# A state-space stage re-pipelined over three periods in a fixed order of TensorE and VectorE, its power products in fewer, longer VectorE operations

## The chip, the cores and the metric

The kernel runs on one core of one Trainium2 chip. A core has a matrix engine (TensorE, PE in the profile), a vector engine (VectorE, DVE), an activation engine (ScalarE, ACT), a general one (GpSimd, POOL) and one whose queue issues most transfers (SyncE, SP). Each takes its instructions in order; they wait for one another through semaphores. The metric is the device time of one execution in microseconds (us), median of several runs.

## What is computed

The reference is a trunk of two layers on x (512 positions, 1024 features, float32). Each normalises x, scales and shifts it by a condition, applies a mixer and adds the gated result. Layer 1's mixer is a gated DeltaNet, which the change doesn't touch. Layer 0's is a state-space mixer of 128 groups with 16 channels and 64 complex states each, cut to what matters:

```
u, z = split(h @ w_in)                      # 1024 -> 2 x 2048
dt = exp(log_dt); a = exp(lam * dt)         # complex; 64 states per group
bb = ((a - 1) / lam) * b                    # complex
x[t] = a * x[t-1] + bb @ u[t]               # per group, 512 positions
y = real(c @ x) + d * u
y = gelu(y); y = y * sigmoid(y @ w_glu); y = y * silu(z); out = y @ w_out
```

## The kernel before

Wide products (`mm3`, L90 to L93) run on TensorE as three passes over a pair of high and low parts: hi·hi, hi·lo, lo·hi. Each weight tile `wraw` (512 KB) is loaded by SP, rounded to `whi` by ScalarE (L78), and VectorE forms the remainder `wlo` (L79).

The kernel's part before 66.5 us makes h and the first eight column tiles of u. Then comes the state-space stage, up to about 429 us. It weaves two things. The first are 40 *units* (`unit`, L497): 24 column tiles of w_in (u to memory, then z through Silu and to memory) and 16 of the first half of w_glu. A unit is eight *fill steps* of three 128x512 matmuls each. Unit 24 on need the gelu of the first eight tiles of y (`p`), split in hi and lo (`yAhi`, `yAlo`); they are loaded back from memory, and their gelu runs, all eight together, at unit 23 (L499 to L505).

The second are sixteen *steps*, each for eight groups. The four positions of a block of four are folded into the contraction, so the recurrence runs over 128 blocks with a to the power 4. A step has
- `s5_prep` (L359): `bl`, the input products: powers of a (`wt`, two pieces loaded from `wd`) times b (`bB`), on GpSimd (L373 to L376), masked by ScalarE (L379); `ca`, the output products `xs`, `xt` of c and powers `pw` on VectorE, six operations of 256 elements (L393 to L398), copied to `cl` by ScalarE; the angles `tau`, on ScalarE (L408), reduced to a fraction in two VectorE operations (L409, L410), then sine and cosine on ScalarE; every fourth step `s5_quad`, the tile `bb` (six VectorE operations).
- `s5_front` (L419): the matmuls `v` of bl and u (L427), on VectorE the rotation into the frame of the decaying modulus (L434, L435), sums (L436, L437), two scans (L439), the rotation back (L442, L443) and the state `st` (L444, L445).
- `s5_back` (L449): the matmuls `y` of ca and state (L457), `kc` on VectorE, `kin` on ScalarE, the transposes `kt` (L467), their copies `tl` on ScalarE (L470), `out` (the product within a block, L473), `yb` and its store to `yd`.

The loop (L531 to L552) puts four units ahead, then in each of 17 periods sixteen fill steps, with the previous step's kt and out and this step's v among them. This order is the order of the program; the order on each engine is made from it by the tile scheduler, which moves instructions by its own cost estimates. After the loop the sixteen fill steps that are left run to the end (`fill(400)`), then the second half of y is loaded, put through gelu (`load_gelu`, L489) and split; its first matmul is `ps_g`.

Of the kernel before, what the change touches and what calls it, by code (L numbers as in the profile page):

```python
# [18 lines left out]
P = 128  # L19
T = 512  # L20
# [21 lines left out]
def hybrid_kernel(ctx: ExitStack, tc: tile.TileContext, a, out, dbg=None):  # L42
# [26 lines left out]
    eps_c, hpi_c = cols[:, 0:1], cols[:, 1:2]  # L69
# [77 lines left out]
    wd = dpool.tile([2, 4, 2, 64, 64], F32, name="wd")  # L147
# [19 lines left out]
    pw = sp.tile([P, 4, 2, 64], F32, name="pw")  # L167
# [9 lines left out]
    def s5_params():  # L177
# [53 lines left out]
        V.tensor_copy(qT[:, 0:2, :], vq[:, :, 64:P])  # L231
        V.tensor_scalar(out=qT[:, 2, :], in0=vq[:, 0, 64:P], scalar1=-1.0, scalar2=None, op0=ALU.mult)
        V.memset(vq[:, 0, 64:P], 1.0)
        V.memset(vq[:, 1, 64:P], 0.0)
        V.tensor_copy(pw[:, 0], vq[:, :, 64:P])
        ta = tmp2()
        tb = tmp2()
        for e in range(1, 5):
            v2 = tmp2()
            V.tensor_tensor(out=ta, in0=vq, in1=av[:, 0:1, :].to_broadcast([P, 2, P]), op=ALU.mult)  # L240
            V.tensor_tensor(out=tb, in0=vq, in1=av[:, 1:2, :].to_broadcast([P, 2, P]), op=ALU.mult)
            V.tensor_tensor(out=v2[:, 0, :], in0=ta[:, 0, :], in1=tb[:, 1, :], op=ALU.subtract)
# [69 lines left out]
    cl = [zz.tile([P, 2, 4, P], F32, name=f"cl{i}") for i in range(2)]  # L312
# [9 lines left out]
    def big(m):  # L322
        ps = psm.tile([P, T], F32, tag="mm", name="ps_mm")
        whi, wlo = load_w(a["winb"][m - 8])
        for k in range(KT):
            mm3(ps, whi[:, k * P:(k + 1) * P], wlo[:, k * P:(k + 1) * P], hhi[:, k, :], hlo[:, k, :],
                k == 0, k == KT - 1)
            if k < KT - 1:
                yield
        if m < 16:  # L330
            put_u(m, ps)
        else:
            z = up.tile([P, T], F32, tag="u", name="z")
            big.last = S.activation(out=z, in_=ps, func=AF.Silu).ins
            SY.dma_start(szd[m - 16], z)

    quad = {}

    def s5_quad(n):
        cC = s5.tile([P, 2, 16, 16], F32, tag="cC", name="cC")  # L340
        bT = s5.tile([P, 2, 16, 16], F32, tag="bT", name="bT", bufs=1)
# [11 lines left out]
        for c in range(2):
            V.tensor_tensor(out=ys[0], in0=bT[:, c], in1=q_b((0, 2)[c]), op=ALU.mult)
            V.tensor_tensor(out=ys[1], in0=bT[:, 1 - c], in1=q_b(1), op=ALU.mult)
            V.tensor_tensor(out=bb[:, c], in0=ys[0], in1=ys[1], op=ALU.subtract)
        return cC, dm, bb

    def s5_prep(i):  # L359
        par = i % 2  # L360
        if i % 4 == 0:
            quad[0] = s5_quad(i // 4)
        cC, dm, bb = quad[0]
        q4 = slice(4 * (i % 4), 4 * (i % 4) + 4)
        wt = s5.tile([P, 2, 256], F32, tag="wt", name="wt", bufs=1)
        for c in range(2):
            SY.dma_start(wt[:, c, :], wd[c].rearrange("j g q n -> (j g) (q n)")[:, 256 * i:256 * i + 256]
                         .unsqueeze(1).to_broadcast([8, 16, 256]))
        bB = s5.tile([P, 2, 256], F32, tag="bB", name="bB")
        SY.dma_start(bB, a["bB"].rearrange("p (c n) -> p c n", c=2)[:, :, 256 * i:256 * i + 256])  # L370
# [6 lines left out]
        bl = s5.tile([P, 2, 4, 2, 64], F32, tag="bl", name="bl")  # L377
        for g in range(2):
            S.activation(out=bl[:, :, :, g, :], in_=ta.rearrange("p c (q n) -> p c q n", n=64), func=AF.Copy,  # L379
                         scale=gmask[g])  # L380

        qs = slice(4 * i, 4 * i + 4)
        pwv = pw[:, :, :, qs].rearrange("p e c q -> p c q e")

        def c_b(c):
            return cC[:, c, q4, :].unsqueeze(2).to_broadcast([P, 4, 4, 16])

        def p_b(c):
# [5 lines left out]
        V.tensor_tensor(out=xt[:, 0], in0=c_b(1), in1=p_b(1), op=ALU.mult)
        V.tensor_tensor(out=xs[:, 0], in0=xs[:, 0], in1=xt[:, 0], op=ALU.subtract)
        V.tensor_tensor(out=xs[:, 1], in0=c_b(0), in1=p_b(1), op=ALU.mult)
        V.tensor_tensor(out=xt[:, 1], in0=c_b(1), in1=p_b(0), op=ALU.mult)
        V.tensor_tensor(out=xs[:, 1], in0=xs[:, 1], in1=xt[:, 1], op=ALU.add)  # L398
        for g in range(2):
            r = slice(64 * g, 64 * g + 64)  # L400
            S.copy(cl[par].rearrange("p c q (e g m) -> p c (q e) g m", e=4, g=2)[r, :, :, g, :],
                   xs[r].rearrange("p c q e m -> p c (q e) m"))
        S.copy(st[par][:, :, :, P:], bb[:, :, q4, :])

        tau = s5.tile([P, 4, P], F32, tag="tau", name="tau", bufs=1)
        kr = s5.tile([P, 4, P], F32, tag="kr", name="kr", bufs=1)
        for q in range(4):
            S.activation(out=tau[:, q, :], in_=iota, func=AF.Copy, scale=t4[:, 4 * i + q:4 * i + q + 1])  # L408
        V.tensor_scalar(out=kr, in0=tau, scalar1=RND, scalar2=RND, op0=ALU.add, op1=ALU.subtract)  # L409
        V.tensor_tensor(out=tau, in0=tau, in1=kr, op=ALU.subtract)  # L410
        tc_ = s5.tile([P, 4, P], F32, tag="tcos", name="tcos")
        ts_ = s5.tile([P, 4, P], F32, tag="tsin", name="tsin")
        S.activation(out=ts_, in_=tau, func=AF.Sin, scale=TWO_PI_LO)
        S.activation(out=kr, in_=tau, func=AF.Abs)
        S.activation(out=tc_, in_=kr, func=AF.Sin, scale=-TWO_PI_LO, bias=hpi_c)
        S.copy(r4t[par][:, :, 1:P], r4[:, qs].unsqueeze(2).to_broadcast([P, 4, P - 1]))
        return bl, tc_, ts_, dm[:, q4, :]

    def s5_front(i, bl, tcs, tsn):  # L419
        par = i % 2  # L420
        U = s5.tile([P, 4, P], F32, tag="U", name="U")
        for j in range(4):
            SY.dma_start(U[32 * j:32 * j + 32], ud[i].rearrange("(q r) (j b) -> j r q b", r=32, j=4)[j])
        psv = ps5.tile([P, 2, 4, P], F32, tag="v", name="ps_v")
        for c in range(2):
            for q in range(4):
                TE.matmul(psv[:, c, q, :], bl[:, c, q].rearrange("p g n -> p (g n)"), U[:, q, :], start=(q == 0), stop=(q == 3))  # L427
        za = s5.tile([P, 2, 4, P], F32, tag="za", name="za")
        zb = s5.tile([P, 2, 4, P], F32, tag="zb", name="zb", bufs=1)

        def flat(x):
            return x.rearrange("p q b -> p (q b)")
# [16 lines left out]
    def s5_back(i, U, dm):  # L449
# [16 lines left out]
        for q in range(4):  # L466
            TE.transpose(pkt[:, q, :], kin[:, q, :], ident)  # L467
# [783 lines left out]
```

## Time and profile before

| | |
|---|---|
| median of 3 runs | 1128.05 us (1125.78 to 1132.82) |
| the profiled execution | 1119.82 us |
| its span in the trace | 1118.1 us |
| TensorE busy | 1052.9 us, 94% |
| VectorE busy | 795.4 us, 71% |
| ScalarE busy | 572.6 us, 51% |
| GpSimd busy | 150.9 us, 13% |

The profile is of one execution. Its span runs from the first to the last instruction; the execution's time is 1.7 us longer. A window's row gives each engine's busy time in it, how many instructions, the clock granted to TensorE as a share of its full speed, the share of the DMA engines' time and what they moved. In a timeline a row gives start, duration, engine and line, operation, output and inputs, and in brackets how long the engine had been idle and for what it waited. The rows stand in a section of their own, below.

### The profile page before, as it was taken

Reading aid. Unit: us, or ns where it says so; the run is one execution under the profiler, and the core shown is the slowest. Engines: PE = TensorE matmul, PEld = TensorE weight load, DVE = VectorE, ACT = ScalarE, POOL = GpSimd, SP = SyncE. Lnnn points to the kernel's source line nnn. Section 1 sums busy time; section 2 is a strip of 40 time slices with the busy share of each in tenths; the row PEclk is TensorE's granted clock in tenths of the full one; section 3 lists DMA queues with packets and bytes.
Section 4 is the critical chain, followed back from the end, with each engine's and each line's share of the span. In section 5 each row is a group of like instructions: output and inputs, shape, how many; then the busy total and the mean of one; then the engine's idle time right before and its main releaser. Section 6 shows DMA issues by size and latency. Waiting matters only on the chain. (4 is left out here: it accounts for less than half of the span.)

```text
span 1118.1 us, 15281 instructions
## 1 busy us (share of the span) xinstructions
PE 1052.9 (94%) x5620; PEld 878.5 (79%) x5620; DVE 795.4 (71%) x1264; ACT 572.6 (51%) x1132; POOL 150.9 (13%) x126
## 2 busy tenths in 40 slices
PE   7997798888889999999999999999999999999997
PEld 5886677777768887888889877778888888887887
DVE  5998999999998747666777578679962344557253
ACT  4565576666877446333445556743343554434241
POOL 0014543232231000000001004220020000200000
PEclk9998899999999999999999999999998999999998
DMA  7766555545332349867664053232251101123342
GB/s 297 265 214 190 144 170 154 171 140 176 95 122 76 114 123 312 303 229 242 209 206 146 15 180 113 68 102 95 83 163 39 39 20 38 57 67 108 99 141 76
DMA packets 80316, 156.57 MB, mean 140 GB/s; under 512 B 9713, under 2 KB 39281, under 8 KB 80242
## 3 DMA queue, kind: packets, MB, share of 16 engines
q1 hardware_dynamic: 79234, 152.45, 41.7%
q0 software_dynamic: 1008, 3.15, 1.1%
q8 instruction: 44, 0.72, 0.3%
q14 instruction: 30, 0.25, 0.1%
HBM read 136.96 MB, written 18.61 MB: 139 GB/s over the span
## 5 line engine op out<-in xcount | busy, mean ns | idle before, releaser
L79 DVE TENSOR_TENSOR wlo<-wraw,whi 128x1024 fp32r<-128x1024 f32 (+1 forms) x141 | 173.0, 1227 | 120.5 <-ACT whi L78 107.3
L78 ACT CAST whi<-wraw 128x1024 fp32r<-128x1024 f32 (+1 forms) x141 | 141.0, 1000 | 209.3 <-PE ps_mm L92 88.3
L91 PE MATMUL ps_mm<-g_hhi,whi 128*128 128x512 f32 x360 | 149.0, 414 | 0.4 <-ACT whi L78 0.4
L92 PE MATMUL ps_mm<-g_hlo,whi 128*128 128x512 f32 x360 | 148.1, 411 | 0.0
L93 PE MATMUL ps_mm<-g_hhi,wlo 128*128 128x512 f32 x360 | 146.7, 408 | 0.5 <-DVE wlo L79 0.5
L93 PEld LDWEIGHTS ps_mm<-g_hhi,wlo 128*128 128x128 f32 x360 | 68.3, 190 | 14.7 <-DVE wlo L79 1.0
L91 PEld LDWEIGHTS ps_mm<-g_hhi,whi 128*128 128x128 f32 x360 | 68.2, 190 | 14.3 <-ACT whi L78 0.8
L91 PE MATMUL ps_mm<-hhi,whi 128*128 128x512 f32 x192 | 78.5, 409 | 0.0
L92 PEld LDWEIGHTS ps_mm<-g_hlo,whi 128*128 128x128 f32 x360 | 68.4, 190 | 12.7
L92 PE MATMUL ps_mm<-hlo,whi 128*128 128x512 f32 x192 | 75.9, 395 | 0.0
L93 PE MATMUL ps_mm<-hhi,wlo 128*128 128x512 f32 x192 | 75.3, 392 | 0.0
L457 PE MATMUL ps_y<-st,cl 128*128 128x144 f32 x256 | 43.9, 326 | 25.6 <-DVE st L444 24.1
L739 DVE SCALAR_TENSOR_TENSOR ac<-ps_mm,cw,ac 128x509 f32<-128x509 f32 (+2 forms) x87 | 64.8, 745 | 3.6 <-ACT ac L736 2.9
L457 PEld LDWEIGHTS ps_y<-st,cl 128*128 128x128 f32 x256 | 38.6, 216 | 33.1 <-issue 25.5
L102 DVE SCALAR_TENSOR_TENSOR adaw<-adaw,cact 128x1024 f32<-128x1024 f32 x48 | 58.8, 1229 | 5.1 <-DMA adaw<-in_adaw_dram 5.1
L128 POOL TENSOR_TENSOR rc<-rc,mhalf 128x2 f32<-128x2 f32 (+1 forms) x5 | 4.8, 960 | 391.8 <-DVE rc L127 378.0
L91 PE MATMUL ps_g<-yBhi,whi 128*128 128x512 f32 x128 | 50.7, 398 | 2.3 <-ACT yBhi L78 2.3
L91 PE MATMUL ps_gh<-yAhi,whi 128*128 128x512 f32 x128 | 51.7, 404 | 0.0
L93 PE MATMUL ps_g<-yBhi,wlo 128*128 128x512 f32 x128 | 50.5, 394 | 0.5 <-DVE wlo L79 0.5
L92 PE MATMUL ps_g<-yBlo,whi 128*128 128x512 f32 x128 | 50.4, 394 | 0.0
L92 PE MATMUL ps_gh<-yAlo,whi 128*128 128x512 f32 x128 | 50.2, 392 | 0.0
L93 PE MATMUL ps_gh<-yAhi,wlo 128*128 128x512 f32 x128 | 50.2, 392 | 0.0
(339 smaller groups left out, 2587.1 us busy)
## 6 DMA issues: line engine op xcount, KB each, us to landing
adaw<-in_adaw_dram SPq DMA_DIRECT2D x48, 512.0 KB
wraw<-in_wginb_dram SPq DMA_DIRECT2D x45, 512.0 KB
wraw<-in_wglu_dram SPq DMA_DIRECT2D x32, 512.0 KB
wraw<-in_winb_dram SPq DMA_DIRECT2D x24, 512.0 KB
wraw<-in_s5o_a_dram SPq DMA_DIRECT2D x16, 384.0 KB
wraw<-in_wgo_a_dram SPq DMA_DIRECT2D x16, 384.0 KB
wraw<-in_wina_dram SPq DMA_DIRECT2D x8, 512.0 KB
bB<-in_bB_dram SPq DMA_DIRECT2D x16, 256.0 KB
```

Source lines behind the costliest of these rows:

```text
L78: S.copy(hi, src)
L79: V.tensor_tensor(out=lo, in0=src, in1=hi.bitcast(F32), op=ALU.subtract)
L91: TE.matmul(ps, whi, xhi, start=start, stop=False)
L92: TE.matmul(ps, whi, xlo, start=False, stop=False)
L93: TE.matmul(ps, wlo, xhi, start=False, stop=stop)
L102: return V.scalar_tensor_tensor(out=aw, in0=aw, scalar=1.0, in1=cact, op0=ALU.mult, op1=ALU.mult, accum_out=mods[:, n:n + 1]).ins
L128: G.tensor_tensor(out=rc[:, 0:n], in0=rc[:, 0:n], in1=mhalf[:, 0:n], op=ALU.pow)
L457: TE.matmul(psy[q // 2][:, q % 2, :], cl[par][:, c, q, :], st[par][:, c, q, :], start=(q % 2 == 0 and c == 0), stop=(q % 2 == 1 and c == 1))
L739: V.scalar_tensor_tensor(out=ac[:, d:], in0=ps[:, 0:T - d], scalar=cw[:, n, k:k + 1], in1=ac[:, d:], op0=ALU.mult, op1=ALU.add)
```

## The change

The order of TensorE's and VectorE's instructions in the stage's loop is fixed by hand (`tc.manual_schedule`); ScalarE, SP and GpSimd are still ordered by the scheduler. A period now works on three steps: y, kt and out of the previous one, rotation, scan and state of the current one, and bl, fraction, sine, cosine, v and ca of the next. The bl products are three VectorE operations of 512 elements in place of four GpSimd ones; a third piece of `wt` and of `bB` (384 KB instead of 256) makes the sign part of the data. ca is three operations of 512, bb likewise. The rounding of the angle is an Identity activation with a bias on ScalarE, and the fraction one VectorE operation. Five units stand ahead of the first step instead of four, so that eight fill steps are left after the loop. Each tile `p` of the first half is loaded back in its own step instead of all at unit 23. U has three buffers instead of two; weight remainders and the casts have places in the order by hand. The diff, cut to its core:

```diff
-        wt = s5.tile([P, 2, 256], F32, tag="wt", name="wt", bufs=1)
+        s.wt = s5.tile([P, 3, 256], F32, tag="wt", name="wt", bufs=1)
...
-        G.tensor_tensor(out=ta, in0=bB, in1=wt[:, 0:1, :].to_broadcast([P, 2, 256]), op=ALU.mult)
-        G.tensor_tensor(out=tb, in0=bB, in1=wt[:, 1:2, :].to_broadcast([P, 2, 256]), op=ALU.mult)
-        G.tensor_tensor(out=ta[:, 0, :], in0=ta[:, 0, :], in1=tb[:, 1, :], op=ALU.subtract)
-        G.tensor_tensor(out=ta[:, 1, :], in0=ta[:, 1, :], in1=tb[:, 0, :], op=ALU.add)
+        V.tensor_tensor(out=ta, in0=s.bB[:, 0:2, :], in1=s.wt[:, 0:1, :].to_broadcast([P, 2, 256]), op=ALU.mult)
+        V.tensor_tensor(out=tb, in0=s.bB[:, 1:3, :], in1=s.wt[:, 1:3, :], op=ALU.mult)
+        V.tensor_tensor(out=ta, in0=ta, in1=tb, op=ALU.add)
...
-        V.tensor_scalar(out=kr, in0=tau, scalar1=RND, scalar2=RND, op0=ALU.add, op1=ALU.subtract)
-        V.tensor_tensor(out=tau, in0=tau, in1=kr, op=ALU.subtract)
+        S.activation(out=s.kr, in_=s.tau, func=AF.Identity, bias=rnd_c)
+    def s5_frac(s):
+        V.scalar_tensor_tensor(out=s.tau, in0=s.kr, scalar=RND, in1=s.tau, op0=ALU.subtract, op1=ALU.subtract)
...
-                for k in range(8):
-                    SY.dma_start(slot(8 + k), yd[k])
+        if s.i < 8:
+            SY.dma_start(slot(8 + s.i), yd[s.i])
...
-    fill(8 * 3)
+    fill(40)
...
+    with tc.manual_schedule(engines={mybir.EngineType.PE, mybir.EngineType.DVE}):
+        for i in range(17):
+            nxt = s5_load(i + 1) if i < 15 else None
+            if i in (1, 5, 9):
+                s5_quad((i + 3) // 4)
+            if prev:
+                s5_y(prev)
+            if cur:
+                s5_rot(cur)
+            fill(3)
+            if prev:
+                s5_kin(prev)
+            if cur:
+                s5_add(cur)
+                s5_cl(cur)
+            fill(1)
+            next_lo()
+            if prev:
+                s5_kt(prev)
+            if i == 9:
+                gelu_a(range(8))
+            if nxt:
+                s5_frac(nxt)
+                s5_bl(nxt)
+            fill(2)
+            if nxt:
+                s5_mask(nxt)
+            if cur:
+                s5_scan(cur)
+            fill(2)
+            unit_end()
+            if prev:
+                s5_out(prev)
+            if cur:
+                s5_unrot(cur)
+            fill(4)
+            if nxt:
+                s5_sincos(nxt)
+                s5_side(nxt)
+            if i < 14:
+                s5_angle(steps[i + 2])
+            if nxt:
+                s5_v(nxt)
+            if cur:
+                s5_state(cur)
+            next_lo()
+            if nxt:
+                s5_ca(nxt)
+            if i in (1, 5, 9):
+                s5_quad_b((i + 3) // 4)
+            fill(4)
+            unit_end()
+            prev, cur = cur, nxt
```

VectorE's order before, in one period of the middle of the stage (`za` and `zb` are the rotated products, `xs` and `xt` ca's products, `kc` the product within a block, `wlo` a weight remainder):

```order
L434 TENSOR_TENSOR za<-ps_v,tcos 128x1024
L435 TENSOR_TENSOR zb<-ps_v,tsin 128x1024
L393 TENSOR_TENSOR xs<-cC,pw 128x256
L436 TENSOR_TENSOR za<-za,zb 128x512
L437 TENSOR_TENSOR za<-za,zb 128x512
L395 TENSOR_TENSOR xs<-xs,xt 128x256
L439 SCALAR_TENSOR_TENSOR zb<-r4t_579,za 128x512 x2
L396 TENSOR_TENSOR xs<-cC,pw 128x256
L442 TENSOR_TENSOR zc<-zb,tcos 128x1024
L398 TENSOR_TENSOR xs<-xs,xt 128x256
L443 TENSOR_TENSOR zb<-zb,tsin 128x1024
L79 TENSOR_TENSOR wlo<-wraw,whi 128x1024
```

And after the change, at the same place, from rotation to back-rotation (the state, a second remainder and ca's three operations of 512 follow):

```order
L523 TENSOR_TENSOR za<-ps_v,tcos 128x1024
L524 TENSOR_TENSOR zb<-ps_v,tsin 128x1024
L558 TENSOR_TENSOR kc<-ps_y,dm 128x32 x2
L527 TENSOR_TENSOR za<-za,zb 128x512
L528 TENSOR_TENSOR za<-za,zb 128x512
L346 TENSOR_TENSOR wlo<-wraw,whi 128x1024
L461 SCALAR_TENSOR_TENSOR tau<-kr,tau 128x512
L479 TENSOR_TENSOR ta<-bB,wt 128x512
L480 TENSOR_TENSOR tb<-bB,wt 128x512
L481 TENSOR_TENSOR ta<-ta,tb 128x512
L532 SCALAR_TENSOR_TENSOR zb<-r4t_579,za 128x512 x2
L537 TENSOR_TENSOR zc<-zb,tcos 128x1024
```

ca has left the chain from the rotation to the state; kc, a remainder, the fraction and the three bl products stand between the sums and the scans instead. On ScalarE, before, the gelu of the first half stand together behind one load of the function table, with the casts of the split behind them:

```order
L505 ACT_TABLE_LOAD
L505 ACTIVATE p_2477<-p_2477 128x512
L505 ACTIVATE p_2479<-p_2479 128x512
L505 ACTIVATE p_2481<-p_2481 128x512
L505 ACTIVATE p_2483<-p_2483 128x512
L505 ACTIVATE p_2485<-p_2485 128x512
L505 ACTIVATE p_2487<-p_2487 128x512
L78 CAST yAhi<-p_2477 128x512
```

After, although the code writes all eight at i = 9, the scheduler puts one into each of the periods 2 to 9, and each has a table load ahead of it and one behind it, before the next Silu of z; this is the second of them:

```order
L560 ACTIVATE kin<-kc,cst 128x16x16 x2
L352 ACT_TABLE_LOAD
L352 ACTIVATE p_1346<-p_1346 128x512
L569 COPY tl_575<-ps_kt 32x512
L569 COPY tl_575<-ps_kt 32x4x96
L569 COPY tl_575<-ps_kt 32x4x64
L569 COPY tl_575<-ps_kt 32x4x32
L487 ACTIVATE bl<-ta,cst 128x8x64 x2
L368 ACT_TABLE_LOAD
L368 ACTIVATE z<-ps_mm 128x512
```

The gelu moved from one place into eight, each ahead of the copies of tl.

## Rows read from the trace of the kernel before

**Rows 1.** The page: the span, and each engine's busy time, share and instructions.
```profile
span 1118.1 us, 15281 instructions
PE 1052.9 (94%) x5620; PEld 878.5 (79%) x5620; DVE 795.4 (71%) x1264; ACT 572.6 (51%) x1132; POOL 150.9 (13%) x126
```

**Rows 2.** Windows of a contended and of the last full period; columns in the first line.
```profile
core 0: us, PE busy (x) PEld busy (x) DVE busy (x) ACT busy (x) POOL busy (x), PEclk, DMA share, GB/s
215.60:234.70 19.10, 16.85 (x92) 13.96 (x93) 17.95 (x23) 12.38 (x25) 5.41 (x4) 1.00 0.55 165
385.30:401.40 16.10, 16.10 (x94) 14.04 (x93) 12.29 (x14) 6.34 (x12) 0.00 (x0) 1.00 0.29 83
```

**Rows 3.** Waits from 60 to 424: total us, times, longest us.
```profile
PE ps_y L457 <- DVE st L444: 24.1, 12, 4.8
```

**Rows 4.** Timeline of TensorE: start, duration; in brackets the idle before.
```profile
96.05 3.78 PE L427 MATMUL ps_v<-U,bl 128*128 128x128 f32 x16 [7.10 <-ACT bl L379]
...
385.29 2.12 PE L457 MATMUL ps_y<-st,cl 128*128 128x144 f32 x16
...
398.63 0.39 PE L91 MATMUL ps_gh<-yAhi,whi 128*128 128x512 f32 x1
...
399.31 0.39 PE L91 MATMUL ps_gh<-yAhi,whi 128*128 128x512 f32 x1
...
401.36 2.12 PE L457 MATMUL ps_y<-st,cl 128*128 128x144 f32 x16
...
429.00 1.14 PE L91 MATMUL ps_g<-yBhi,whi 128*128 128x512 f32 x2 [2.31 <-ACT yBhi L78]
```

**Rows 5.** Timeline of GpSimd: the second product at the head, two of a contended period.
```profile
90.76 2.33 POOL L374 TENSOR_TENSOR tb<-bB,wt 128x512 f32<-128x512 f32 x1 [1.67 <-DMA wt<-wd]
...
222.85 1.75 POOL L373 TENSOR_TENSOR ta<-bB,wt 128x512 f32<-128x512 f32 x1 [9.06 <-ACT bl L379]
...
231.15 1.73 POOL L374 TENSOR_TENSOR tb<-bB,wt 128x512 f32<-128x512 f32 x1 [4.54 <-DMA wt<-wd]
```

**Rows 6.** Timeline of VectorE in the contended period.
```profile
223.37 1.78 DVE L437 TENSOR_TENSOR za<-za,zb 128x512 f32<-128x512 f32 x1
225.07 0.95 DVE L395 TENSOR_TENSOR xs<-xs,xt 128x256 f32<-128x256 f32 x1
225.94 2.87 DVE L439 TENSOR_TENSOR_SCAN zb<-r4t,za 128x512 f32<-128x512 f32 x2
...
231.65 2.31 DVE L79 TENSOR_TENSOR wlo<-wraw,whi 128x1024 fp32r<-128x1024 f32 x1
```

**Rows 7.** Timeline of VectorE undisturbed: a ca product, and the last full period.
```profile
158.81 0.42 DVE L397 TENSOR_TENSOR xt<-cC,pw 128x256 f32<-128x256 f32 x1
...
387.48 0.28 DVE L460 TENSOR_TENSOR kc<-ps_y,dm 128x32 f32<-128x32 f32 x2
389.23 1.23 DVE L434 TENSOR_TENSOR za<-ps_v,tcos 128x1024 f32<-128x1024 f32 x1 [1.47 <-PE ps_v L427]
...
391.62 0.69 DVE L436 TENSOR_TENSOR za<-za,zb 128x512 f32<-128x512 f32 x1
392.23 0.69 DVE L437 TENSOR_TENSOR za<-za,zb 128x512 f32<-128x512 f32 x1
392.95 2.34 DVE L439 TENSOR_TENSOR_SCAN zb<-r4t,za 128x512 f32<-128x512 f32 x2
...
399.05 1.22 DVE L79 TENSOR_TENSOR wlo<-wraw,whi 128x1024 fp32r<-128x1024 f32 x1
```

**Rows 8.** Timeline of ScalarE: a table load and what follows, and a gelu.
```profile
411.75 1.28 ACT L606 ACT_TABLE_LOAD   x1
413.05 0.63 ACT L606 ACTIVATE yr<-yr 128x512 f32<-128x512 f32 x1
...
419.81 2.61 ACT L491 ACTIVATE yG<-yG 128x512 f32<-128x512 f32 x4 [2.61 <-DMA yG<-yd]
```

**Rows 9.** Timeline of SP's queue: the loads of the second half of y.
```profile
414.35 4.59 SPq L490 DMA_DIRECT2D yG<-yd  x8
```

More of the change, by code (lines that the diff above doesn't have):

```diff
@@ L311, in hybrid_kernel @@
     zz = sB.enter_context(tc.tile_pool(name="zz", bufs=1, reuse_waits="tile"))
-    cl = [zz.tile([P, 2, 4, P], F32, name=f"cl{i}") for i in range(2)]
+    cl = [zz.tile([P, 4, 2, P], F32, name=f"cl{i}") for i in range(2)]
     tl = [zz.tile([P, 4, P], F32, name=f"tl{i}") for i in range(2)]
@@ new lines, in next_lo, with gelu_a, split_y @@
+    def next_lo():
+        n = lo_next[0]
+        if n in pairs:
+            hi, lo = pairs[n]
+            V.tensor_tensor(out=lo, in0=raws.pop(n), in1=hi.bitcast(F32), op=ALU.subtract)
+            get_raw(n + 2)
+            lo_next[0] += 1
+    def gelu_a(ks):
+        for k in ks:
+            S.activation(out=part[8 + k], in_=part[8 + k], func=AF.Gelu_apprx_tanh)
+    yAx = ExitStack()
+    yA = []
+    def split_y(k):
+        split(part[8 + k], yA[0][:, k, :], yA[1][:, k, :])
+    ends = []
@@ new lines, in unit_end, with unit @@
+    def unit_end():
+        for n, ps in ends:
+            if n < 8:
+                put_u(8 + n, ps)
+            elif n < 24:
+                z = up.tile([P, T], F32, tag="u", name="z")
+                S.activation(out=z, in_=ps, func=AF.Silu)
+                SY.dma_start(szd[n - 8], z)
+            else:
+                S.copy(slot(n - 24), ps)
+            get_hi(n + 2)
+        ends.clear()
+    def unit(n):
+        if n == 24:
+            hB.close()
+            yAp = yAx.enter_context(tc.tile_pool(name="yAp", bufs=1, side="right", reuse_waits="tile"))
+            yA.extend([yAp.tile([P, 8, T], F32R, name="yAhi"), yAp.tile([P, 8, T], F32R, name="yAlo")])
+            split_y(0)
+        ps = psm.tile([P, T], F32, tag="mm", name="ps_mm" if n < 24 else "ps_gh")
+        whi, wlo = pairs.pop(n)
+        xh, xl = (hhi, hlo) if n < 24 else yA
@@ L325, in big @@
         for k in range(KT):
-            mm3(ps, whi[:, k * P:(k + 1) * P], wlo[:, k * P:(k + 1) * P], hhi[:, k, :], hlo[:, k, :],
+            if n == 24 and k < 7:
+                split_y(k + 1)
+            mm3(ps, whi[:, k * P:(k + 1) * P], wlo[:, k * P:(k + 1) * P], xh[:, k, :], xl[:, k, :],
                 k == 0, k == KT - 1)
+            if k == 3 and lo_within[0]:
+                next_lo()
             if k < KT - 1:
                 yield
[L330 to L335, printed above, removed]
+        ends.append((n, ps))
@@ L337, in hybrid_kernel, with units, fill, flat @@
+        if lo_within[0]:
+            unit_end()
+        yield
+    def units():
+        for n in range(40):
+            yield from unit(n)
+    us = units()
+    def fill(n):
+        for _ in range(n):
+            next(us, None)
+    def flat(x):
+        return x.rearrange("p q b -> p (q b)")
+    class Step:
+        def __init__(self, i):
+            self.i, self.par, self.q4 = i, i % 2, slice(4 * (i % 4), 4 * (i % 4) + 4)
+    steps = [Step(i) for i in range(16)]
     quad = {}
@@ L353, in s5_quad @@
[L353 to L364, printed above, removed]
-        wt = s5.tile([P, 2, 256], F32, tag="wt", name="wt", bufs=1)
-        for c in range(2):
-            SY.dma_start(wt[:, c, :], wd[c].rearrange("j g q n -> (j g) (q n)")[:, 256 * i:256 * i + 256]
-                         .unsqueeze(1).to_broadcast([8, 16, 256]))
-        bB = s5.tile([P, 2, 256], F32, tag="bB", name="bB")
-        SY.dma_start(bB, a["bB"].rearrange("p (c n) -> p c n", c=2)[:, :, 256 * i:256 * i + 256])
+        quad[n] = cC, dm, bb, bT
@@ new lines, in s5_quad_b @@
+    def s5_quad_b(n):
+        cC, dm, bb, bT = quad[n]
+        ns = slice(16 * n, 16 * n + 16)
+        ys = [s5.tile([P, 2, 16, 16], F32, tag=f"y{i}", name=f"y{i}", bufs=1) for i in range(2)]
+        V.tensor_tensor(out=ys[0], in0=bT[:, 0:2], in1=qT[:, 0:2, ns].unsqueeze(3).to_broadcast([P, 2, 16, 16]), op=ALU.mult)
+        V.tensor_tensor(out=ys[1], in0=bT[:, 1:3],
+                        in1=qT[:, 2:3, ns].unsqueeze(3).to_broadcast([P, 2, 16, 16]), op=ALU.mult)
+        V.tensor_tensor(out=bb, in0=ys[0], in1=ys[1], op=ALU.subtract)
@@ new lines, in s5_angle @@
+    def s5_angle(s):
+        s.tau = s5.tile([P, 4, P], F32, tag="tau", name="tau", bufs=1)
+        s.kr = s5.tile([P, 4, P], F32, tag="kr", name="kr", bufs=1)
+        for q in range(4):
+            S.activation(out=s.tau[:, q, :], in_=iota, func=AF.Copy, scale=t4[:, 4 * s.i + q:4 * s.i + q + 1])
+        S.activation(out=s.kr, in_=s.tau, func=AF.Identity, bias=rnd_c)
+    def s5_frac(s):
+        V.scalar_tensor_tensor(out=s.tau, in0=s.kr, scalar=RND, in1=s.tau, op0=ALU.subtract, op1=ALU.subtract)
@@ L394, in s5_prep, with s5_ca @@
[L394 to L398, printed above, removed]
+    def s5_ca(s):
+        cC = quad[s.i // 4][0]
+        qs = slice(4 * s.i, 4 * s.i + 4)
+        pwv = pw[:, qs].rearrange("p q c e -> p q (c e)")
+        sh = [P, 4, 8, 16]
+        xs = s5.tile(sh, F32, tag="xs", name="xs", bufs=1)
+        xt = s5.tile(sh, F32, tag="xt", name="xt", bufs=1)
+        for x, c in ((xs, 0), (xt, 1)):
+            V.tensor_tensor(out=x, in0=cC[:, c, s.q4, :].unsqueeze(2).to_broadcast(sh),
+                            in1=pwv[:, :, 4 * c:4 * c + 8].unsqueeze(3).to_broadcast(sh), op=ALU.mult)
+        V.tensor_tensor(out=xs, in0=xs, in1=xt, op=ALU.subtract)
+        s.xs = xs
@@ L399, in s5_prep, with s5_cl @@
+    def s5_cl(s):
         for g in range(2):
             r = slice(64 * g, 64 * g + 64)
[L401 to L408, printed above, removed]
@@ L417, in s5_prep @@
[L417 to L424, printed above, removed]
+            S.copy(cl[s.par].rearrange("p q c (e g m) -> p (q c e) g m", e=4, g=2)[r, :, g, :],
+                   s.xs[r].rearrange("p q x m -> p (q x) m"))
@@ L520, in units @@
-    def units():
-        for n in range(40):
-            yield from unit(n)
-            yield
-    us = units()
-    def fill(n):
-        for _ in range(n):
-            next(us, None)
-    fill(8 * 3)
-    s5_params()
-    back = None
-    for i in range(17):
-        if i < 16:
-            *pre, dm = s5_prep(i)
-            if i == 0:
-                fill(8)
-        if back is not None:
-            next(back)
-        if i < 16:
-            U = s5_front(i, *pre)
-        fill(3)
-        if back is not None:
-            next(back)
-        fill(3)
-        if back is not None:
-            next(back, None)
-        fill(10)
-        if i < 16:
-            back = s5_back(i, U, dm)
@@ L564, in hybrid_kernel, with glu_half @@
             split(load_gelu(8 + k, yGp.tile([P, T], F32, name=f"yG{k}")), yBhi[:, k, :], yBlo[:, k, :])
+    def glu_half(m, hf, ps, yh, yl):
+        whi, wlo = load_w(a["wglu"][2 * m + hf])
+        for k in range(8):
+            mm3(ps, whi[:, k * P:(k + 1) * P], wlo[:, k * P:(k + 1) * P], yh[:, k, :], yl[:, k, :], k == 0, k == 7)
+            if k < 7:
+                yield
     gHx = ExitStack()
```

225 lines of the change are left out of this document (122 added, 103 removed).

## The prediction

> **What bounds the kernel now.** I read the page first: one core, a span of 1118.1 us, TensorE busy for 94% of it and VectorE for 71% [rows 1]. Averages hide the stage that the change touches, the state-space stage, which I take from the first rotation (99.83, the end of the first v) to the last y (401.36) and on to 429.00, where the part that the diff leaves alone begins [rows 4]. So next came the busy time by windows [rows 2]. A typical period between two y's lasts 19.10 us; TensorE is busy for 16.85 of it, VectorE for 17.95, ScalarE for 12.38, GpSimd for 5.41. In the last full period, where no preparation is left and GpSimd does nothing, the same sixteen fill steps and the same small matmuls fit into 16.10 with TensorE busy throughout. So TensorE could go at about 16.07 (385.29 to 401.36, without a wait) [rows 4] and goes at 19. The waits say for whom: in twelve periods y waited 24.1 us in all for VectorE's states [rows 3]. VectorE closes the loop; of the 19.10 it has 1.15 left, and what it does decides the period.
>
> The timelines of VectorE show two things. In a quiet period rotation, sums, scan, back-rotation and state follow one another from 389.23 to 399.05 without a gap worth a line: 9.82 us [rows 7]. In a contended one the same instructions are longer: a sum 1.78 for 0.69, the ca sum 0.95 for the 0.42 of another ca operation of its size, the pair of scans 2.87 for 2.34, the weight remainder wlo 2.31 for 1.22 [rows 6, 7]. Together 1.09 + 0.53 + 0.53 + 1.09 = 3.24 us in this period, and GpSimd's two products lie on exactly these instants (222.85 and 231.15) [rows 5].
>
> **The change part by part.** I make the sum on the profiled execution (1119.82; the median of the runs shown is 1128.05) and subtract the gain from the median.
>
> VectorE's period in its new order. A 512-element operation starts 0.61 after the one before it (391.62 to 392.23, duration 0.69), so ends overlap by 0.08 [rows 7].
> - Rotation to state: 9.82.
> - Two weight remainders at 1.22 - 0.08 = 1.14: 2.28.
> - Two kc: 0.28.
> - The fraction of the angle, now one operation with the rounding moved to ScalarE: 0.61.
> - The three bl products, from GpSimd: 3 x 0.61 = 1.83.
> - ca, three of 512 for six of 256: 1.83.
>
> The sum is **16.65**. It goes by uncontended durations, since no product stands on GpSimd any more. One thing has no row: the new bl and ca products read broadcast operands of 512 elements. The bounds are no extra at all and the full duration of 0.69 without overlap, 0.5 a period; I take nothing, because the ca product of 256 at 158.81 has such operands and takes 0.42, on the line from 0.28 (two kc) to 0.69 [rows 7].
>
> From the first rotation to the last state there were 399.05 - 99.83 = 299.2 us. After: fifteen periods of 16.65 (249.8), the last chain of 9.82 + 0.28 + 1.14 = 11.2, three bb preparations of 3 x 0.61 (5.5) and the eight remainders of the first half's gelu output, 8 x 0.61 (4.9), which lie in this stretch before and after: 271.4. **Gain 27.8**, if TensorE and ScalarE keep up.
>
> TensorE has 16.07 of work in 16.65, so 0.58 of room. In the new order kt stands four fill steps (2.7 us) behind y, and out and the next v again four each, so kc, kin and tl have that long. By the durations this just suffices.
>
> The head. Before, v(0) began at 96.05 after a wait of 7.10 for bl [rows 4], which came from GpSimd: its second product began at 90.76 when wt landed [rows 5]. After, five units stand ahead instead of four; eight fill steps of 0.68 (398.63 to 399.31) cover 5.4 of the 7.1, until 94.4. VectorE needs from the landing 0.7 + 0.7, and ScalarE's two masks 2 x 0.63 (a 512-element operation there) [rows 8]: 93.4. But a third wt piece is loaded, and it stands on SP behind the weight loads; it may cost nothing or what the products on GpSimd took, 2.3 [rows 5]. I take the middle, 94.55: **1.5 gained**, between 0 and 4.
>
> The tail. State(15) ended at 399.05 and y began at 401.36; y would go at once (2.3), and eight fill steps fewer are left behind it (5.4). Both take cover from the gelu of the second half: its loads were issued at 414.35 [rows 9], the first gelu began at 419.81 after 2.61 of waiting [rows 8], and TensorE still waited 2.31 at 429.00 [rows 4]. Of the 7.7 I take 3 as given back to this, between 0 and 7.7: **4.7 gained**.
>
> ScalarE gets 0.63 per period for the rounding. The gelu of the first half, until now eight in a row behind one table load, are now spread: one per period in eight periods, and each brings a switch of the function table there and one back. A switch is 1.30 from the load at 411.75 to the next activation at 413.05 [rows 8]. So ScalarE's period is 12.38 + 0.63 + 0.63 + 2.60 = 16.2, still below 16.65, but the copies of tl stand behind the gelu, and the gelu waits for its own tile to come back from memory, 5.46 from issue to use at 414.35 to 419.81. I cost it at nothing, with 16.65 - 16.2 = 0.4 as its cover. If that is not enough, out is late, and then the output of the step and the tile that a later gelu waits for.
>
> What the Trainium skill says on the switch stands apart from the sum. Its page "ScalarE: Activation LUTs", section "What ACT_TABLE_LOAD costs", gives 1283 ns for the load plus about 1380 ns of drain, 2.66 us per switch. The trace agrees with the load alone: the next activation began 1.30 behind it, and no drain is seen there. By the page ScalarE would need 18.95 in these eight periods, 2.3 too many in each, and the time would be 1112.
>
> The sum: 27.8 + 1.5 + 4.7 = 34.0, so 1119.82 - 34.0 = 1085.8 for the profiled execution, and 1128.05 - 34.0 = **1094** for the median.
>
> **The rivals.**
> - TensorE sets the period, because VectorE's bb preparations, the remainders and some small operations fall into gaps: 15 x 0.58 = 8.7 less, and up to 10.4 more if the 5.5 and 4.9 hide too. 1075 to 1085. For it: the quiet period reaches 16.07. Against: VectorE has no gap in the sum to hide them in.
> - ScalarE sets the eight gelu periods. With the gelu's tile late, out is held in every one of them; at 17.25 a period (0.6 more) 5 us come on top, 1099; with switches twice as dear as the row (each the load and as long again, 16.2 + 2.6 = 18.8) 8 x 2.15 = 17 come on top, 1111. For it: tl is behind the gelu on the same engine. Against: the row of the switch.
> - TensorE waits at kt in every period, because kc stands behind the rotation on VectorE and kin behind ScalarE's other work. Each microsecond costs 15 to 16 us; the gain is gone at 34.0 / 16 = 2.1 us per period. Between 1117 and 1139. For it: a fixed order cannot let later work pass a late one. Against: outside the gelu periods ScalarE is busy for 13.0 of 16.65.
> - **The other side:** what stretches VectorE is not GpSimd but something that stays. The transfers are a candidate: in the quiet period the DMA share was 0.29, in the contended one 0.55 [rows 2], and the new kernel moves the same weights in less time. Then 3.24 x 15 = 48.6 come back, and the time is 1094 + 48.6 = 1142.6. It decides where more than (34.0 + 11.3) / 15 = 3.0 of the 3.24 stays. Against: the long instructions coincide with GpSimd's products, not with a change in transfers.
>
> **How the numbers follow.** VectorE paces, 1086 to 1099: 0.55. TensorE paces, 1074 to 1086: 0.12. ScalarE paces part of it, 1099 to 1113: 0.18. TensorE held at kt, within 1% (about what a measurement of this kernel can tell from no change): 0.09. The stretch stays, slower by over 1%: 0.06. So faster by over 1% 0.85, same 0.09, slower 0.06. The time is that of the likeliest case, 1094; the range takes in the first three cases, 1074 to 1113, and leaves out 0.15.
>
> **What would show it.** Right: no tensor operation on GpSimd between 66 and 400; the second sum of the rotation at 0.69 and every remainder at 1.22; two v's about 16.65 apart with VectorE over 95% busy between them; y no longer waits for states, and TensorE's waits of about half a microsecond per period fall on kt or out; v(0) before 95; the switches at 1.30 each with tl behind them. The sum is wrong in the term of contention if the sums stay at 1.8, in the term of ScalarE if out waits for tl by more than a microsecond in the gelu periods, and in that of the tail if the wait at the first ps_g grows far beyond 2.31 + 3.

## The result, and the profile after

The new kernel takes 1088.4 us (median of 4 runs, 1086.08 to 1090.24), the kernel before 1127.9 beside it; the ratio is 0.9643, with a 95% interval of 0.9604 to 0.9682. In a later comparison it was 1085.8 against 1124.4, 0.9669 (0.9640 to 0.9698). The forecast was 1094, between 1074 and 1113: the time lies in the range and in the case held likeliest. The profiled execution took 1086.08; the sum had made 1085.8 of it. The median is a further 5.6 us below the forecast because the two profiled executions lie differently in their spreads: that of the kernel before 8.2 us below the 1128.05 that the sum was taken from, that of the new kernel 2.3 below its 1088.4. In the later comparisons the runs of the kernel before spread from 1118 to 1131, those of the new kernel from 1083 to 1090.

The page, answering [rows 1]:

```profile
span 1084.4 us, 15225 instructions
PE 1041.8 (96%) x5620; PEld 869.5 (80%) x5620; DVE 774.9 (71%) x1246; ACT 599.8 (55%) x1163; POOL 57.5 (5%) x62
```

Windows of the new kernel, a period with a gelu and one without (columns as in [rows 2]):

```profile
151.26:167.75 16.49, 16.29 (x92) 13.62 (x92) 16.32 (x23) 14.97 (x28) 0.00 (x0) 1.00 0.70 201
...
312.67:329.16 16.49, 16.40 (x95) 13.96 (x94) 16.32 (x22) 12.92 (x26) 0.00 (x0) 1.00 0.49 144
```

Both last 16.49, from rotation to rotation, and VectorE is busy for 16.32. GpSimd does nothing. The DMA share of 0.70 is higher than the 0.55 of the contended period of [rows 2]. VectorE's timeline in that period:

```profile
151.26 1.22 DVE L523 TENSOR_TENSOR za<-ps_v,tcos 128x1024 f32<-128x1024 f32 x1
152.39 1.22 DVE L524 TENSOR_TENSOR zb<-ps_v,tsin 128x1024 f32<-128x1024 f32 x1
153.52 0.28 DVE L558 TENSOR_TENSOR kc<-ps_y,dm 128x32 f32<-128x32 f32 x2
153.72 0.68 DVE L527 TENSOR_TENSOR za<-za,zb 128x512 f32<-128x512 f32 x1
154.32 0.68 DVE L528 TENSOR_TENSOR za<-za,zb 128x512 f32<-128x512 f32 x1
154.92 1.21 DVE L346 TENSOR_TENSOR wlo<-wraw,whi 128x1024 fp32r<-128x1024 f32 x1
156.06 0.68 DVE L461 SCALAR_TENSOR_TENSOR tau<-kr,tau 128x512 f32<-128x512 f32 x1
156.66 0.68 DVE L479 TENSOR_TENSOR ta<-bB,wt 128x512 f32<-128x512 f32 x1
157.26 0.68 DVE L480 TENSOR_TENSOR tb<-bB,wt 128x512 f32<-128x512 f32 x1
157.98 0.69 DVE L481 TENSOR_TENSOR ta<-ta,tb 128x512 f32<-128x512 f32 x1
158.59 2.33 DVE L532 TENSOR_TENSOR_SCAN zb<-r4t,za 128x512 f32<-128x512 f32 x2
```

Each begins as the one before it ends, or just ahead of that; the second sum takes 0.68 where [rows 6] had 1.78, the remainder 1.21 where they had 2.31. From the first rotation (99.94) to the last state (373.01) it took 273.1 us; before, 299.2.

### The profile page after: what moved, and what is told of

Same layout as the page of the kernel before. It is cut to its first block, busy times and chain, and to the rows that moved or that the text cites. A ratio compares the mean times of both kernels' runs of the same rounds, so it can differ in the third digit from the quotient of the medians.

```text
span 1084.4 us, 15225 instructions
## 1 busy us (share of the span) xinstructions
PE 1041.8 (96%) x5620; PEld 869.5 (80%) x5620; DVE 774.9 (71%) x1246; ACT 599.8 (55%) x1163; POOL 57.5 (5%) x62
## 5 line engine op out<-in xcount | busy, mean ns | idle before, releaser
L79 ACT CAST whi<-wraw 128x1024 fp32r<-128x1024 f32 (+1 forms) x101 | 99.1, 981 | 175.8 <-PE ps_mm L93 74.9
L80 DVE TENSOR_TENSOR wlo<-wraw,whi 128x1024 fp32r<-128x1024 f32 (+1 forms) x101 | 116.1, 1149 | 92.9 <-ACT whi L79 79.6
L346 DVE TENSOR_TENSOR wlo<-wraw,whi 128x1024 fp32r<-128x1024 f32 x40 | 48.7, 1219 | 10.8 <-ACT whi L340 10.8
L340 ACT CAST whi<-wraw 128x1024 fp32r<-128x1024 f32 x40 | 41.8, 1044 | 24.2 <-issue 7.7
L94 PEld LDWEIGHTS ps_mm<-hhi,wlo 128*128 128x128 f32 x192 | 36.4, 190 | 8.2
```

Source lines behind the costliest of these rows:

```text
L79: S.copy(hi, src)
L80: V.tensor_tensor(out=lo, in0=src, in1=hi.bitcast(F32), op=ALU.subtract)
L94: TE.matmul(ps, wlo, xhi, start=False, stop=stop)
L340: S.copy(pairs[n][0], raws[n])
L346: V.tensor_tensor(out=lo, in0=raws.pop(n), in1=hi.bitcast(F32), op=ALU.subtract)
```

## The experiments

The theory: operations of GpSimd stretch those of VectorE, and VectorE's work sets the period. Its rivals: the order is what counts; something else stretches VectorE (transfers); TensorE or ScalarE paces.

**One part undone: the bl products back on GpSimd, in the new order.**

```diff
-        V.tensor_tensor(out=ta, in0=s.bB[:, 0:2, :], ...
-        V.tensor_tensor(out=tb, in0=s.bB[:, 1:3, :], ...
-        V.tensor_tensor(out=ta, in0=ta, in1=tb, op=ALU.add)
+        G.tensor_tensor(out=ta, in0=s.bB[:, 0:2, :], ...
+        G.tensor_tensor(out=tb, in0=s.bB[:, 1:3, :], ...
+        G.tensor_tensor(out=ta, in0=ta, in1=tb, op=ALU.add)
```

> The new order, but the three bl products of each period on GpSimd instead of VectorE. Theory (GpSimd's products stretch VectorE's operations, VectorE paces): the VectorE period of 16.48 loses three operations of 0.61 (1.83) and gains a stretch of about 3.2, so about 17.8 and 1088.4 + 15 x 1.4 = about 1109; sums and remainders that lie beside a product take up to 1.8 and 2.3 instead of 0.69 and 1.22. Rival (the stretch was not GpSimd's): VectorE has 14.65 to do, TensorE paces at 16.07, about 1082, and all VectorE durations stay as they are.

It took 1132.75, 0.5% more than the kernel before (ratio 1.0054, 1.0026 to 1.0083). VectorE's groups between 100 and 370 (mean ns behind the busy time) and the waits from 60 to 400:

```profile
L523 DVE TENSOR_TENSOR za<-ps_v,tcos 128x1024 f32<-128x1024 f32 x14 | 17.0, 1218 | 12.4 <-PE ps_v L514 12.4
L528 DVE TENSOR_TENSOR za<-za,zb 128x512 f32<-128x512 f32 x13 | 13.3, 1020 | 0.0
...
ACT bl L487 <- POOL ta L481: 38.5, 7, 10.6
...
PE ps_kt L566 <- ACT kin L560: 23.5, 7, 7.4
```

The stretch is back (the second sum 1.02 on average for 0.68), as the theory says and the rival doesn't. But 1109 was expected, and 24 more came. From 66.5 to the first ps_g the row is this (that of the new kernel stands further down):

```profile
66.50:436.15 369.65, 323.81 (x1666) 272.56 (x1664) 299.70 (x355) 261.23 (x475) 76.71 (x48) 0.93 0.52 153
```

Against the new kernel's 330.60 and 291.45, VectorE is busy only 8 us more (three products fewer per period, the rest longer) and idle 31 us more: here it does not pace. The masks on ScalarE wait up to 10.6 us for GpSimd, kin behind them comes late, and TensorE waits 23.5 us at kt. This is not the late products alone: the scheduler, which still orders ScalarE, put a sine between gelu and Silu in every gelu period, so ScalarE has 25 table loads in the loop instead of 18, 9 us of loads more. Which of the two makes how much of the 24 is not shown.

**One part alone: the kernel before with only its bl products on VectorE.** The old loop, the scheduler's order, ca in six pieces, four units ahead.

```diff
-        G.tensor_tensor(out=ta, in0=bB, in1=wt[:, 0:1, :]...
+        V.tensor_tensor(out=ta, in0=bB, in1=wt[:, 0:1, :]...
...
```

> The kernel before, with only its four bl products moved from GpSimd to VectorE; the scheduler orders everything as before. Theory (the stretch is about 3.2 of the period, and the waits of about 1.1 come from the order): VectorE's period becomes 17.95 - 3.24 + 1.9 to 2.5, with the waits about 18, so 15 to 18 us faster than before, 1110 to 1113. Rival one (the order is what counts): no faster than 1125. Rival two (the stretch is all): 1095 or less.

It took **1085.4**, ratio 0.9633 (0.9591 to 0.9676): all of the change's gain, from moving four operations; the second rival holds. A period from y to y, the waits from 60 to 400, and a few rows of VectorE's timeline:

```profile
214.23:231.22 16.99, 16.27 (x93) 13.83 (x92) 16.99 (x29) 13.41 (x26) 0.00 (x0) 1.00 0.65 199
```
```profile
PE ps_y L457 <- DVE st L444: 4.1, 6, 1.2
```
```profile
222.03 0.68 DVE L436 TENSOR_TENSOR za<-za,zb 128x512 f32<-128x512 f32 x1
222.63 0.68 DVE L437 TENSOR_TENSOR za<-za,zb 128x512 f32<-128x512 f32 x1
223.23 0.68 DVE L373 TENSOR_TENSOR ta<-bB,wt 128x512 f32<-128x512 f32 x1
```

VectorE is busy for the whole 16.99, and the waits of y for states fell from the 24.1 of [rows 3] to 4.1. My expectation kept 1.1 us of idle per period as belonging to the order. That was wrong: VectorE's idle time went with the stretch.

**The fixed order taken away from the new kernel.**

```diff
-    with tc.manual_schedule(engines={mybir.EngineType.PE, mybir.EngineType.DVE}):
+    if True:
```

> The new kernel without the fixed order: the same program, but TensorE's and VectorE's instructions are ordered by the scheduler again. Theory (the order itself is worth the waits of about 1.1 per period, the rest is the removed stretch): 1100 to 1110. Rival (the order of writing already gives it): 1086 to 1091.

It took 1086.0 (0.9648, 0.9591 to 0.9706). The rival holds: the fixed order is worth nothing that can be measured.

**Is it contention, or that bl came late from GpSimd?** The kernel before, with bl on VectorE and the same four operations also on GpSimd, for nobody.

```diff
+        G.tensor_tensor(out=tc2, in0=bB, in1=wt[:, 0:1, :]...
+        G.tensor_tensor(out=td2, in0=bB, in1=wt[:, 1:2, :]...
+        G.tensor_tensor(out=tc2[:, 0, :], in0=tc2[:, 0, :], in1=td2[:, 1, :], op=ALU.subtract)
+        G.tensor_tensor(out=tc2[:, 1, :], in0=tc2[:, 1, :], in1=td2[:, 0, :], op=ALU.add)
```

> The kernel before with its four bl products on VectorE (as in the run that made it as fast as the change), and the same four operations once more on GpSimd, at their old places, into tiles that nothing reads. Theory (GpSimd's operations stretch VectorE's, whoever needs their results): the stretch of about 3.2 per period comes back on top of VectorE's 17.0, so about 20.2 and 1085 + 48 = 1125 to 1135. Rival (the products came late from GpSimd, and the stretch is a detail): nothing waits for GpSimd here, so 1085 to 1095.

It took 1132.2 (ratio 1.0083, 1.0060 to 1.0106): 47 us more than the run without these four operations per step, whose results nothing uses. One of the idle products and the sum beside it, then VectorE's groups between 100 and 400:

```profile
160.09 1.53 POOL L379 TENSOR_TENSOR tc<-bB,wt 128x512 f32<-128x512 f32 x1 [12.06 <-issue]
```
```profile
160.39 1.78 DVE L442 TENSOR_TENSOR za<-za,zb 128x512 f32<-128x512 f32 x1
```
```profile
L445 DVE TENSOR_TENSOR_SCAN zb<-r4t,za 128x512 f32<-128x512 f32 x30 | 45.0, 1539 | 0.0
...
L448 DVE TENSOR_TENSOR zc<-zb,tcos 128x1024 f32<-128x1024 f32 x15 | 22.0, 1467 | 0.0
...
L440 DVE TENSOR_TENSOR za<-ps_v,tcos 128x1024 f32<-128x1024 f32 x15 | 18.3, 1218 | 2.7 <-PE ps_v L433 2.5
```

The sum takes 1.78 beside the product, 0.68 elsewhere. A scan takes 1.54 on average (1.21 in the new kernel), the back-rotation 1.47 for 1.23. The rotation, which reads the same amount, stays at 1.22. The windows from 66.5 to the first ps_g, of the run with bl on VectorE alone and of this one:

```profile
66.50:394.46 327.96, 312.23 (x1669) 261.69 (x1667) 297.84 (x492) 231.05 (x445) 0.00 (x0) 0.99 0.53 167
```
```profile
66.50:442.49 375.99, 328.07 (x1667) 276.58 (x1665) 341.48 (x488) 230.04 (x443) 100.91 (x64) 0.94 0.46 141
```

The second is 48.0 longer; VectorE is busy 43.6 of them and idle 4.4. From the first rotation to the last state its instructions are the same and in the same order in both runs, and for wt it waits only 1.1 us between 100 and 400. This decides it: contention is enough for the whole difference, without a product that is late.

**The price of a GpSimd product in the new order.** Two idle products per period.

```diff
+                for _ in range(2):
+                    G.tensor_tensor(out=<the tile y1>, in0=nxt.bB[:, 0:2, :], in1=nxt.bB[:, 1:3, :], op=ALU.mult)
```

> The new kernel with two extra 512-element products per period on GpSimd, from bB into a tile that nothing uses (16 periods' worth of 15). Theory (stretch by GpSimd): VectorE is busy all the time, so both products lie on its operations; each costs it 1.1 to 1.6, the period becomes 18.7 to 19.7 and the time 1121 to 1136. Rival (the stretch came from transfers or from something else that stays): no change, 1086 to 1091.

It took 1105.4 (0.9802, 0.9759 to 0.9846), 17 to 20 more than the new kernel (1088.4 and 1085.8): the right sign, half of the size. One pair, on GpSimd and on VectorE:

```profile
157.06 3.05 POOL L634 TENSOR_TENSOR y<-bB 128x512 f32<-128x512 f32 x2 [9.51 <-DMA bB<-in_bB_dram]
```
```profile
157.28 1.67 DVE L501 TENSOR_TENSOR xs<-xs,xt 128x512 f32<-128x512 f32 x1
158.88 1.21 DVE L523 TENSOR_TENSOR za<-ps_v,tcos 128x1024 f32<-128x1024 f32 x1
```

The first product costs the ca sum 0.98 (1.67 for 0.69). The second lies beside the rotation and costs nothing. I had taken each product to cost 1.1 to 1.6, wherever it falls.

**Who paces the new kernel?** Two sums left out of VectorE's period.

```diff
-        V.tensor_tensor(out=xs, in0=xs, in1=xt, op=ALU.subtract)
-        V.tensor_tensor(out=ta, in0=ta, in1=tb, op=ALU.add)
```

> The new kernel without two VectorE operations per period (the sum of the bl products and that of the ca products are left out, so the output is not the reference's). Theory (VectorE paces at 16.48, TensorE could do 16.07): VectorE's period falls to 15.27, TensorE's to 16.1 to 16.3; with part of the bb preparations hidden 6 to 9 us faster than the new kernel, 1080 to 1083. Rival (TensorE or ScalarE paces already): no more than 2 us, 1086 to 1090.

1080.5, in the range of the theory; a period late in the stage:

```profile
318.03:334.13 16.10, 16.10 (x93) 14.04 (x92) 15.11 (x20) 12.96 (x27) 0.00 (x0) 1.00 0.45 139
```

With 1.2 us less for VectorE the period falls by 0.38 and TensorE is busy throughout. So VectorE paces the new kernel, by 0.4 us per period, with TensorE right behind.

**What the table loads cost.** The eight gelu left out of the loop.

```diff
-            if i == 9:
-                gelu_a(range(8))
```

> The new kernel without the eight gelu of the first half inside the loop (left out, so the output is not the reference's); the sixteen table loads around them go too. Theory (VectorE paces, ScalarE has room even with the switches): VectorE lost about 0.9 us in the seven gelu periods and some 3 in the one after them, so 1 to 4 us faster, 1084 to 1088. Rival (ScalarE paces the eight periods, with 2.66 per switch): 15 to 18 us faster, 1070 to 1073.

1083.5, as the theory says. Seventeen table loads (in one period a sine stands between gelu and Silu and adds one) and eight gelu together cost 2 to 5 us (against 1085.8 and 1088.4; the profiled spans are 1079.9 and 1084.4); the rival's 15 is excluded. In the new kernel, ScalarE's timeline shows a switch in place:

```profile
153.84 0.91 ACT L560 ACTIVATE kin<-kc,cst 128x256 f32<-128x256 f32 x2
154.76 1.28 ACT L352 ACT_TABLE_LOAD   x1
156.06 0.63 ACT L352 ACTIVATE p<-p 128x512 f32<-128x512 f32 x1
```

**Four units ahead instead of five.** `fill(32)` for `fill(40)`.

> The new kernel with four units ahead of the first step instead of five. Theory (the first v waits for the third piece of wt, which lands at about 93.6 whatever stands ahead; the unit that is moved only fills this wait): the first rotation stays at about 100, eight fill steps of 0.68 more stand in the tail, 3 to 5 us slower, 1091 to 1094. Rival (the fifth unit delays the first step and the tail hides the rest): the same or faster, 1084 to 1088.

1092.6, 4 to 7 more than the new kernel, as expected: the last operation on the state began at 368.90 and the first ps_g at 399.53, 30.6 later, against 24.7 with five units (372.42 to 397.11).

**The third piece of wt at the first step.** It is not loaded but made from the second.

```diff
-        for c in range(3):
+        for c in range(2 if i == 0 else 3):
...
+            V.tensor_scalar(out=s.wt[:, 2, :], in0=s.wt[:, 1, :], scalar1=-1.0, scalar2=None, op0=ALU.mult)
```

> The new kernel, where the third piece of the first step's wt is not loaded but made by VectorE from the second (one more operation). Theory (the first v waits 2.59 us for a product that waited 3.02 for this piece): the first v begins as soon as TensorE gets there, at about 94, and the first rotation at 97.3 to 98 instead of 99.94; 2 to 2.6 us faster. Rival (the second piece or u lands no earlier): no change within 1 us.

1088.3, beside 1085.8 for the new kernel run with it: no gain. The two spreads overlap (1086.1 to 1090.5, 1083.1 to 1089.9).

> The new kernel as it is, for comparison on the same chip: 1086 to 1091.

Its first v began at 94.86 this time, and not at 96.47 as in the first profile, and without the third piece at 94.77. What followed was worse:

```profile
104.38 1.05 ACT L340 CAST whi<-wraw 128x1024 fp32r<-128x1024 f32 x1 [8.25 <-DMA wraw<-in_winb_dram]
...
109.05 1.22 PE L516 MATMUL ps_v<-U,bl 128*128 128x128 f32 x4 [4.03 <-ACT bl L489]
```

ScalarE stood 8.25 us before a cast whose weights had not landed, with the second step's masks behind it, so the second v waited 4.03. The head hangs on several transfers at once: between the two profiled executions of the new kernel the first rotation moved by 3.0 us (99.94 and 96.95).

**Two attempts at a faster kernel.** Without the fixed order and the third piece:

> The new kernel without the fixed order and without the load of the third piece at the first step. Theory (the two are independent; the order is worth nothing): 1083 to 1086. Rival (the scheduler's order loses what the head gains): 1086 to 1090.

1086.5 (0.9663, 0.9637 to 0.9690): no better. And the same with the eight gelu in one batch:

> As the run before, with the eight gelu of the first half together behind the last Silu of z, as the kernel before has them. Theory (the gelu with their switches cost about 4.5 when spread; in one block they hold kin and the masks once for some 6 us, of which TensorE's fill steps cover most): 1080 to 1085. Rival (kin behind the block stops TensorE): 1086 to 1092.

1094.5 (0.9741, 0.9715 to 0.9766): worse. From one rotation to the next it took 28.7 us at the batch (271.92 to 300.60). No version ran that beats both; the old order with bl on VectorE equals the new kernel with a far smaller edit.

## Why the prediction was right

**The sum came out nearer than its terms.** In the profiled executions the gain was 33.7 us against 34.0, but by cancellation: the stage gave 26.1 for 27.8, the head -0.1 for 1.5, the tail 5.9 for 4.7, and 1.8 came behind the first ps_g, where the sum had nothing. That it hit within 0.3 is luck; the mechanism (VectorE's period without the stretch) is what the runs bear out.

**VectorE's period: right.** The sum said 16.65, the trace shows 16.49. The difference is overlap between operations, which I had counted for some and not for all. The short terms (three products of 0.61, one fraction of 0.61, three ca operations) are there row by row, and the broadcast operands cost nothing. Over fifteen periods the 0.16 makes 2.4 us; some 4 us of waiting, most of it where the w_glu units begin, took them back.

**One reading was loose.** The prediction laid all four long instructions on GpSimd's two products. The ca sum (225.07) and the scans (225.94) lie beside GpSimd's two sums instead:

```profile
224.67 1.06 POOL L375 TENSOR_TENSOR ta<-ta,tb 128x256 f32<-128x256 f32 x1
225.69 0.92 POOL L376 TENSOR_TENSOR ta<-ta,tb 128x256 f32<-128x256 f32 x1
```

The stretch is GpSimd's all the same.

**What the gain is made of: only half seen.** I forecast a new order with a new sum, and its 27.8 came out as 26.1. But I never asked what the old order would give without the stretch. It gives 17.0 in the period shown and the same time. From 66.5 to the first ps_g the rest of the change saves VectorE 6.4 us of work (297.84 to 291.45) and gives back 9.0 in idle time (30.1 to 39.2), so the first ps_g comes at 397.11 in the new kernel and at 394.46 in the old order with bl on VectorE. From the first rotation to the last state, with the same number of fill steps, the new kernel takes 273.1 and that run 265.4 (99.73 to 365.14); the tail, with eight fill steps fewer, makes up most of it. Nor is the idle 1.15 us per period of [rows 2] a flaw of the order, as two of my expectations had it: it went when the stretch went. The stretch itself can be summed by the groups' means. From 66.5 on in the stage, of the kernel before (window, then VectorE's groups: busy, mean ns):

```profile
66.50:429.00 362.50, 320.71 (x1668) 269.00 (x1666) 314.90 (x428) 229.85 (x445) 93.43 (x64) 0.96 0.49 150
...
L79 DVE TENSOR_TENSOR wlo<-wraw,whi 128x1024 fp32r<-128x1024 f32 x40 | 55.2, 1381 | 28.6 <-ACT whi L78 28.6
...
L437 DVE TENSOR_TENSOR za<-za,zb 128x512 f32<-128x512 f32 x16 | 19.6, 1228 | 0.0
```

and the same of the new kernel:

```profile
66.50:397.10 330.60, 312.47 (x1665) 263.96 (x1663) 291.45 (x403) 251.76 (x468) 0.00 (x0) 0.98 0.57 171
...
L346 DVE TENSOR_TENSOR wlo<-wraw,whi 128x1024 fp32r<-128x1024 f32 x40 | 48.7, 1219 | 10.8 <-ACT whi L340 10.8
...
L528 DVE TENSOR_TENSOR za<-za,zb 128x512 f32<-128x512 f32 x16 | 10.9, 682 | 0.0
```

Forty remainders lost 6.5 us, sixteen second sums 8.7, and with all other groups it is about 42. Against it, bl adds 16 x 1.83 = 29 to VectorE, the angle takes some 7 off, and ca and bb in half as many operations some 3. Its busy time fell by 23.5, from 314.9 to 291.45, its idle time by 8.4, from 47.6 to 39.2. TensorE's granted clock is no part of the period's difference: it is 1.00, the higher of its two levels, in the contended period of [rows 2] and in both periods of the new kernel.

**The head: the term failed.** I took 1.5 of gain (0 to 4). The trace shows -0.1:

```profile
93.63 0.69 DVE L480 TENSOR_TENSOR tb<-bB,wt 128x512 f32<-128x512 f32 x1 [3.02 <-DMA wt<-wd]
```
```profile
96.47 3.43 PE L514 MATMUL ps_v<-U,bl 128*128 128x128 f32 x16 [2.59 <-ACT bl L487]
```

The third piece landed 2.9 after the time at which GpSimd's second product had begun before (90.76), beyond my bound of 2.3; in the second profile of the same kernel the first rotation came at 96.95, a gain of 2.9. Both lie in the bounds of 0 to 4 or next to them; the term has no single value.

**The tail: 4.7 forecast, 5.9 measured.** From the last state to the first ps_g it took 24.1 instead of 29.95 (399.05 to 429.00). The wait there became 1.19 where it was 2.31, so I had given back too much to the gelu of the second half:

```profile
397.11 0.50 PE L92 MATMUL ps_g<-yBhi,whi 128*128 128x512 f32 x1 [1.19 <-ACT yBhi L79]
```

**What I had not counted.** Where the w_glu units begin, the period from 253.00 to 279.00 took 26.0: 16.5, a bb preparation of 1.9 and eight remainders of 4.9, which stood in the sum, and 2.7 of waiting on VectorE, which did not. First kc, and the sums behind it, waited for y; then TensorE waited 3.6 for a cast of yAhi (waits from 255 to 285):

```profile
PE ps_gh L92 <- ACT yAhi L79: 3.6, 1, 3.6
...
DVE kc L558 <- PE ps_y L550: 2.7, 3, 1.3
```

**The rivals.** TensorE as the pace: not reached, but only 0.4 us per period away. ScalarE in the gelu periods: it is busy 14.97 of 16.49 where I had added up 16.2, and the gelu with their switches, which I had put at nothing, cost 2 to 5 us, not 17. A switch takes 1.28: the load begins 0.01 behind the instruction ahead of it, and the activation 0.02 behind the load. So the 2.66 us per switch of the Trainium skill (the page "ScalarE: Activation LUTs", section "What ACT_TABLE_LOAD costs") are not seen here; the load alone agrees, 1.28. The late kt: it did not occur in the new kernel (4.4 us of waits in all between 60 and 400) but did in the run with bl on GpSimd, where bl was late and ScalarE had more table loads. The stretch from something that stays: refuted by the DMA share of 0.70 beside undisturbed durations, and by the four idle operations that bring it back.

**What stays open.** Why the runs of the kernel before spread over 13 us and those of the new kernel over 7. The stretch depends on what lies beside GpSimd's products, and these wait for transfers ([rows 5]), so its amount could vary from run to run; no run here tests that.

## What to carry to other kernels

Before an order is rebuilt, look for operations of the busiest engine that take longer in one place than in another, and see who is running beside them; here moving four operations off a third engine gave all that a rewritten pipeline gave. Where one engine's order is fixed and another's is left to the scheduler, look at the other's order again after every edit: seven table loads came in that way. Price an offload to GpSimd by what it does to VectorE, and place it beside operations that it does not disturb. When the sum of the new kernel fits, also make the sum of the old kernel without the one flaw: only the difference is what the rest of the change is worth.

## What the runs showed of the hardware

A GpSimd product that nobody reads stretched a sum on VectorE by 1.10 us (1.78 for 0.68, at 160.39 in the run with the four idle operations), but not all kinds of operation are stretched. The rotation, with one operand from PSUM and one from SBUF, kept 1.22 in every kernel (1218 ns on average both with GpSimd busy for 101 us in the stage and with GpSimd idle), while operations with two operands in SBUF were stretched. The Trainium skill ("SBUF — State Buffer", section "Who interferes with whom") says that a VectorE instruction with at most one SBUF input, outside the two-port modes, does not contend with GpSimd, and that one with two SBUF inputs contends with a GpSimd instruction that reads SBUF; the rows agree, and they show what I had not used: the same GpSimd work is free beside a PSUM-fed operation (the second product of the pair at 157.06) and costs 0.98 beside a sum.
